# A hybrid layer on one core: weight splits on GpSimd, and another order of work at the start

## The chip, the core and the metric

The kernel runs on one core of a Trainium2 chip. A core has five engines with instruction queues of their own, each of which works its queue strictly in the order in which it was written: TensorE (PE in the profile; its weight loads appear apart as PEld), VectorE (DVE), ScalarE (ACT), GpSimd (POOL) and SyncE (SP), which here only issues transfers. Engines wait for one another through semaphores. The metric is the time of one execution in device microseconds (us), as the median of several runs.

## The reference

One layer, 1024 tokens of width 1024, in fp32. What matters here is the front of it:

```
h    = rmsnorm(x, norm1_w)
proj = h @ w_in                     # all columns of both mixers in one product
q, k, v = silu(causal_conv4(...))   # mixer A: gated delta rule, 4 heads of 128
beta, g = gates from 8 columns of proj
o_a  = rmsnorm(chunked delta rule) * silu(z)
o_b  = dilated attention of 8 heads of 64, three (window, dilation) branches
x    = x + concat(o_a, o_b) @ w_out
x    = x + (silu(gate) * up) @ w_down   # after rmsnorm, up-projection, causal conv of width 3
out  = rmsnorm(x, final_norm_w)
```

## The kernel before

**Layout and precision.** Tensors are kept transposed: 128 partitions by 1024 tokens, eight such tiles for the width. Every large fp32 product is made of three products of TensorE. An operand is split into a high part (`hi`, a rounded copy made by ACT) and a low part (`lo`, source minus high part, made by DVE), and `mm3` (line 200) adds high by high, high by low and low by high into one bank of sums. A row `ps<-xhi,whi` is a product with the high part of an input tile and of a weight, `ps<-xhi,wlo` one with the low part of the weight, `ps<-xlo,whi` one with the low part of the input. Each has 128x512 results.

**Helpers.** `Engine` records every operation, so that all operations of DVE, ACT, POOL and SP have one line in the profile: L142, or L144 if they were written through `uv` or `ua`, which raise their priority in the scheduler by `URGENT`. L193 is a product, L197 a transposition on TensorE. `split` (206) makes a high and a low part with `ac` and `ve`, the handles of normal priority.

**Who sets the order.** TensorE's order is written out by a planner, `Weave`: the parts of the layer are generators, each of which says by `need` when its operands should be ready by modelled costs, and the planner takes the first one that is ready. Every product gets an issue token, so the order stays as planned. The order on the other engines is made by a scheduler, from the dependencies, the place in the program and the priority. `after(inst, anchor)` binds an instruction behind another one without any data between them. Pools have a fixed number of buffers per tag; raw weights (`wst`), their high parts (`whi`) and their low parts (`wlo`) have two each.

**The start** (lines 288 to 324, 346 to 348 and 353 to 361). A loop over the eight row blocks k loads `xt` (block k of the transposed input) and, for every second k, a weight piece, and splits both. Each block is also squared by ACT (`sq`), and DVE adds the squares up in `acc`, which the norm needs. Meanwhile TensorE makes 18 warm-up products that nobody reads. Then `first` makes the columns of three key heads: for each k six groups of three products, into six banks. `norms` (367) sums `acc` over the partitions (`ps<-ones,acc`, 128x1 each) and `gates` (388) makes the gates from eight columns (`ps<-xt,wba`); its last step on DVE is `ngam`. `first_keys` then scales the keys (`xr`), convolves them (`kT<-xr,gcw,kT`) and hands them to `kprep`, which makes the decay matrices `dec` (eight ACT operations a head), the tokens-first copies `ktok` and the small vectors around them.

**The dense stage** (`dense`, 485). It works through `DENSE`, a list of columns: the last key head, two halves of the values of mixer B (`V`), then q and v of each head, eight columns of mixer B (`a`) and four gate columns (`z`). `take` hands out the weight that was split before and starts the split of the next one; weight 0 belongs to the key column, 1 to 8 to the values, 9 to 28 to the other twenty. A value weight is used by eight groups of products with the operands exchanged (`ps<-whi,xhi`, `ps<-wlo,xhi`, `ps<-whi,xlo`, in this order), over four banks, and `vx` on ACT empties the four banks at the end of a half. A column of the other kind takes sixteen groups, 48 products. Woven into this stage are the preparation of q and v (`qT`, `vT`, `vtok`), the forward substitution of the delta rule on DVE (`xi`, `tmp`, `mt`; its result reaches TensorE as `x`, `um`), the chain over the chunks, and the attention of mixer B (scores `ps<-kT,qT`, probabilities `pb`, denominators `rd`). Behind it come the output projection and the MLP, which take most of the time and are not touched.

**POOL before.** It clears some tiles, takes powers (`nk`, `rq`, `ms`), masks `dec`, scales `vtok` and copies `rd`: 78 instructions in all.

The diff touches `weight`, `split_x`, the loop of the start, the warm-up, `first` and `take`:

## Time and profile before

| | us |
|---|---|
| median of three runs (lowest, highest) | 1209.37 (1208.98, 1209.37) |
| the profiled execution | 1209.18 |
| its span in the profile | 1207.4 |
| PE busy | 1192.3 |
| DVE busy | 925.8 |
| ACT busy | 576.2 |
| POOL busy | 59.1 |

The mean clock that TensorE was granted is 0.996 of full speed. The span is the time from the first to the last record; what lies around it, 1.8 us, belongs to the execution and not to any engine. Busy times are sums over records. A row of the timeline gives the start, the length and the tiles of an instruction (or of several alike in a row); products overlap in their records, so the distance between two starts, and not the length, is what one product costs. In brackets stands how long the engine was idle before a row, and which engine's work ended that.

### The profile page before, as it was taken

The numbers are of one execution on the slowest core, as the hardware profiler recorded it, in microseconds if no ns is written. First come the engines' busy times: TensorE is split into PE (matmuls) and PEld (weight loads), VectorE is DVE, ScalarE is ACT, GpSimd is POOL, SyncE is SP. The second block draws the span as 40 slices with busy tenths as digits, with TensorE's granted clock in tenths as the row PEclk, the third lists the DMA queues.
The fourth block names the chain that finished last, engine by engine and source line by source line (L and its number), as shares of the span: only waits on it lengthen the run. The fifth ranks groups of instructions, "written<-read, shape, count | busy, mean of one in ns | idle before, by whom it ended". The sixth has DMA issues, their size and how long they took to land.

```text
span 1207.4 us, 18350 instructions
## 1 busy us (share of the span) xinstructions
PE 1192.3 (99%) x7068; PEld 986.6 (82%) x7068; DVE 925.8 (77%) x1470; ACT 576.2 (48%) x1134; POOL 59.1 (5%) x78
## 2 busy tenths in 40 slices
PE   9999999999999999999999999999999999999997
PEld 7887888889877778888888888888888888888886
DVE  7683975666466556768988989889898889999865
ACT  7384335356355443655545445444454454444441
POOL 0211010003211000000000000000000000000000
PEclk9999999999999999999999999999999999999999
DMA  7424343435633213544223132231322298556513
GB/s 230 111 75 125 117 120 108 157 102 167 213 118 119 89 36 100 174 136 157 71 69 105 53 105 82 75 105 53 105 65 93 89 366 311 177 163 226 162 57 140
DMA packets 85798, 154.80 MB, mean 128 GB/s; under 512 B 21168, under 2 KB 36304, under 8 KB 85712
## 3 DMA queue, kind: packets, MB, share of 16 engines
q1 hardware_dynamic: 85136, 153.12, 39.3%
q8 instruction: 55, 0.90, 0.3%
q10 hardware_dynamic: 576, 0.52, 0.1%
q14 instruction: 31, 0.25, 0.1%
HBM read 117.68 MB, written 35.93 MB: 127 GB/s over the span
## 4 chain that ended last, share of the span: by engine, by line
PE 93%; DVE 3%; ACT 2%; issue 1%; DMA 1%; SPq 0%; POOLq 0%; POOL 0%; DVEq 0%; ACTq 0%
PE ps L193 44%; PE pa L193 20%; PE dw L193 17%; PE pc L193 10%; PE ps L197 3%; DVE kT L142 1%; DMA xt<-in_xT 1%; DVE wlo L142 0%; ACT dec L142 0%; DVE xr L142 0%; DVE x1h L142 0%; PE pd L193 0%; DVE qT L142 0%; SPq L142 0%; ACT xr L142 0%
## 5 line engine op out<-in xcount | busy, mean ns | idle before, releaser
L193 PE MATMUL dw<-pr 128*128 128x512 f32 (+1 forms) x984 | 211.3, 376 | 0.0
L193 PEld LDWEIGHTS dw<-pr 128*128 128x128 f32 x984 | 176.7, 188 | 33.6
L193 PE MATMUL ps<-xhi,whi 128*128 128x512 f32 x384 | 157.3, 410 | 0.0
L193 PE MATMUL ps<-xlo,whi 128*128 128x512 f32 x384 | 150.0, 391 | 0.8 <-DVE xlo L142 0.8
L193 PE MATMUL ps<-xhi,wlo 128*128 128x512 f32 x384 | 150.2, 391 | 0.0
L193 PE MATMUL pa<-T,pair 128*128 128x512 f32 x528 | 127.0, 389 | 0.0
L193 PEld LDWEIGHTS pa<-T,pair 128*128 128x128 f32 x528 | 99.0, 188 | 20.5
L193 PEld LDWEIGHTS ps<-xhi,whi 128*128 128x128 f32 x384 | 72.2, 188 | 18.1 <-issue 4.7
L193 PEld LDWEIGHTS ps<-xhi,wlo 128*128 128x128 f32 x384 | 72.1, 188 | 15.7 <-DVE wlo L142 0.2
L193 PEld LDWEIGHTS ps<-xlo,whi 128*128 128x128 f32 x384 | 72.4, 188 | 13.4 <-DVE xlo L142 1.1
L142 ACT ACTIVATE u<-pa 128x512 f32<-128x512 f32 x44 | 26.3, 598 | 107.3 <-PE pa L193 107.3
L142 DVE SCALAR_TENSOR_TENSOR y<-xu,fcw,y 128x1023 f32<-128x1023 f32 (+1 forms) x44 | 56.4, 1281 | 22.1 <-ACT y L142 22.0
L142 ACT ACTIVATE whi<-wst 128x1024 fp32r<-128x1024 f32 (+2 forms) x33 | 33.3, 1009 | 68.0 <-PE ps L193 62.4
L193 PE MATMUL pa<-B,A 128*128 128x512 f32 x264 | 63.4, 389 | 0.0
L193 PE MATMUL pc<-T,S 128*128 128x512 f32 x264 | 63.4, 389 | 0.0
L193 PE MATMUL pa<-T,S 128*128 128x512 f32 x264 | 63.4, 389 | 0.0
L193 PE MATMUL pc<-B,pair 128*128 128x512 f32 x264 | 63.4, 389 | 0.0
L142 DVE TENSOR_TENSOR wst<-wst 128x512 f32<-128x512 f32 x88 | 60.4, 687 | 0.9
L193 PE MATMUL ps<-B,pair 128*128 128x512 f32 x252 | 60.5, 389 | 0.0
L144 ACT ACTIVATE sm<-sm,mx 128x128 f32<-128x128 f32 (+7 forms) x64 | 35.4, 556 | 50.5 <-DVE mx L144 50.5
L193 PEld LDWEIGHTS pa<-T,S 128*128 128x128 f32 x264 | 49.6, 188 | 10.3
L193 PEld LDWEIGHTS pc<-T,S 128*128 128x128 f32 x264 | 49.6, 188 | 10.3
(245 smaller groups left out, 2344.7 us busy)
## 6 DMA issues: line engine op xcount, KB each, us to landing
wst<-in_wu SPq DMA_DIRECT2D x44, 512.0 KB, 3.7
wd<-in_wd SPq DMA_DIRECT2D x44, 512.0 KB, 4.5
upark<-y SPq DMA_DIRECT2D x22, 512.0 KB, 3.7
wst<-in_wi SPq DMA_DIRECT2D x21, 512.0 KB, 3.7
r<-upark SPq DMA_DIRECT2D x11, 512.0 KB, 7.5
r<-upark SPq DMA_DIRECT2D x22, 256.0 KB, 6.8
wa<-in_wd SPq DMA_DIRECT2D x22, 256.0 KB, 3.1
wst<-in_wv SPq DMA_DIRECT2D x8, 512.0 KB, 3.7
```

Of the source, the lines that this page charges most:

```text
L142: return getattr(eng, op)(*a, **kw)
L144: return getattr(eng, op)(*a, **kw)
L193: tc.stamp_issue_order_token(nc.tensor.matmul(dst, lhs, rhs, start=start, stop=stop, **kw).ins, TOKEN)
L197: tc.stamp_issue_order_token(nc.tensor.transpose(dst, src, ident if idt is None else idt).ins, TOKEN)
```

## The change

It has four parts.

1. `weight` has lost its urgent halves. The value weights (1 to 8) are split whole, at normal priority, on ACT and DVE; the twenty weights from 9 on get their low part from POOL instead of DVE.
2. Ten warm-up products instead of eighteen.
3. In `first`, for the first two row blocks, the two products with the high part of the input come ahead of those with its low part (by groups of three for k=0, over all six for k=1). From k=2 on nothing changes.
4. The splits of the start have raised priority, and every square and its addition into `acc` is bound behind the splits of two row blocks later; the last two behind the last splits.

```
@@ -212,14 +212,16 @@
         sy.dma_start(st, src)
         return st
 
-    def weight(src, n=1024, st=None, urgent=False):
+    def weight(src, n=1024, st=None, spare=False):
         if st is None:
             st = raw_weight(src, n)
         hi = tile_(wp, [P, n], F32R, "whi", "whi", 2)
         lo = tile_(wp, [P, n], F32R, "wlo", "wlo", 2)
-        for sl in (half(0), half(1)) if urgent else (slice(0, n),):
-            (ua if urgent else ac).activation(hi[:, sl], st[:, sl], AF.Copy)
-            (uv if urgent else ve).tensor_tensor(lo[:, sl], st[:, sl], hi[:, sl].bitcast(F32), op=OP.subtract)
+        if spare:
+            ac.activation(hi, st, AF.Copy)
+            po_.tensor_tensor(lo, st, hi.bitcast(F32), op=OP.subtract)
+        else:
+            split(st, hi, lo)
         return hi, lo
 
     def wk_by_halves(src):
@@ -281,9 +283,25 @@
 
     def split_x(xt, k, sl):
         hi, lo = xs[k]
-        ac.activation(hi[:, sl], xt[:, sl], AF.Copy, scale=n1[:, k:k + 1])
-        ve.scalar_tensor_tensor(lo[:, sl], xt[:, sl], n1[:, k:k + 1], hi[:, sl].bitcast(F32), op0=OP.mult,
-                                op1=OP.subtract)
+        his[k:] = [ua.activation(hi[:, sl], xt[:, sl], AF.Copy, scale=n1[:, k:k + 1])]
+        lo_of[0] = uv.scalar_tensor_tensor(lo[:, sl], xt[:, sl], n1[:, k:k + 1], hi[:, sl].bitcast(F32), op0=OP.mult,
+                                           op1=OP.subtract)
+
+    def split_first(src, hi, lo):
+        ua.activation(hi, src, AF.Copy)
+        return uv.tensor_tensor(lo, src, hi.bitcast(F32), op=OP.subtract)
+
+    his, los, lo_of, sqs = [], [], [None], []
+
+    def square(k, hi, lo):
+        sq = A("sq", "qa")
+        late = "the products wait for the splits first"
+        after(ac.activation(sq, xts[k], AF.Square), hi, late)
+        sqs.append(sq)
+        if k == 1:
+            after(ve.tensor_tensor(acc, sqs[0], sq, op=OP.add), lo, late)
+        elif k > 1:
+            after(ve.tensor_tensor(acc, acc, sq, op=OP.add), lo, late)
 
     for k in range(KT):
         xt = A("xt", ("kT*", "dv*")[k % 2])
@@ -299,29 +317,22 @@
             for h in range(2):
                 sy.dma_start(xt[:, half(h)], I["xT"][:P, half(h)])
             sy.dma_start(wst[:, 1, :], I["w0"][0, :, 1])
-            split(wst[:, 0, :], whi[:, 0, :], wlo[:, 0, :])
+            split_first(wst[:, 0, :], whi[:, 0, :], wlo[:, 0, :])
             for h in range(2):
                 split_x(xt, 0, half(h))
-            split(wst[:, 1, :], whi[:, 1, :], wlo[:, 1, :])
+            split_first(wst[:, 1, :], whi[:, 1, :], wlo[:, 1, :])
         else:
             if k % 2 == 0:
                 sy.dma_start(wst, I["w0"][k // 2])
             sy.dma_start(xt, I["xT"][k * P:(k + 1) * P, :])
             if k % 2 == 0:
-                wlast = split(wst, whi, wlo)
+                split_first(wst, whi, wlo)
             split_x(xt, k, slice(0, S))
-        sq = A("sq", "qa")
-        ac.activation(sq, xt, AF.Square)
-        if k == 0:
-            sq0 = sq
-        elif k == 1:
-            ve.tensor_tensor(acc, sq0, sq, op=OP.add)
-        else:
-            inst = ve.tensor_tensor(acc, acc, sq, op=OP.add)
-            if k == 6:
-                after(inst, first_lo, "the products wait for these weights")
-        if k == 4:
-            first_lo = wlast
+        los.append(lo_of[0])
+        if k > 1:
+            square(k - 2, his[k], los[k])
+    for k in (KT - 2, KT - 1):
+        square(k, his[-1], los[-1])
 
 
     ident = const("ident", [P, P], I["ident"])
@@ -344,8 +355,8 @@
 
 
     wbank = bank("atr", "warm")
-    for _ in range(18):
-        mm(wbank[:, :P], warm, warm, 0.3)
+    for _ in range(10):
+        mm(wbank[:, :P], warm, warm, 0.43)
 
 
     pst = [bank(t) for t in ("hf", "asc", "ch") for _ in range(2)]
@@ -353,11 +364,24 @@
     def first():
         for k in range(KT):
             w = wk0[k // 2]
-            for i in range(6) if k else (0, 2, 4, 1, 3, 5):
+            if k < 2:
+                for group in ((0, 2, 4), (1, 3, 5)) if k == 0 else (range(6),):
+                    for low in range(2):
+                        for i in group:
+                            m, h = divmod(i, 2)
+                            wm = [t[:, k % 2, m * P:(m + 1) * P] for t in w]
+                            hi, lo = [t[:, half(h)] for t in xs[k]]
+                            if low:
+                                mm(pst[i], wm[0], lo, 0.2135, False, False)
+                            else:
+                                mm(pst[i], wm[0], hi, 0.2135, k == 0, False)
+                                mm(pst[i], wm[1], hi, 0.2135, False, False)
+                continue
+            for i in range(6):
                 yield wv.need(*xs[k], *w)
                 m, h = divmod(i, 2)
                 wm = [t[:, k % 2, m * P:(m + 1) * P] for t in w]
-                mm3(pst[i], wm, [t[:, half(h)] for t in xs[k]], k == 0, k == KT - 1)
+                mm3(pst[i], wm, [t[:, half(h)] for t in xs[k]], False, k == KT - 1)
         wv.done.add("first")
 
 
@@ -513,7 +537,7 @@
             w = nxt.pop()
             i = place[0] = place[0] + 1
             if i < len(srcs):
-                nxt.append(weight(None, st=raw.pop(), urgent=1 <= i <= 8))
+                nxt.append(weight(None, st=raw.pop(), spare=i >= 9))
             if i + 1 < len(srcs):
                 raw.append(raw_weight(srcs[i + 1]))
             return w
```

What this does to the queues is seen at three places. On DVE at the start, the additions into acc stood each right behind its low part; the rows before:

```order
L142 TENSOR_TENSOR wlo<-wst,whi 128x384
L142 TENSOR_SCALAR xlo<-xt,n_72,xhi 128x512 x2
L142 TENSOR_TENSOR wlo<-wst,whi 128x384
L142 TENSOR_SCALAR xlo<-xt,n_72,xhi 128x1024
L142 TENSOR_TENSOR acc<-sq 128x1024
L142 TENSOR_TENSOR wlo<-wst,whi 128x768
L142 TENSOR_SCALAR xlo<-xt,n_72,xhi 128x1024
L142 TENSOR_TENSOR acc<-acc,sq 128x1024
L142 TENSOR_SCALAR xlo<-xt,n_72,xhi 128x1024
L142 TENSOR_TENSOR acc<-acc,sq 128x1024
L142 TENSOR_SCALAR xlo<-xt,n_72,xhi 128x1024
L142 TENSOR_TENSOR acc<-acc,sq 128x1024
```

and the same place after:

```order
L144 TENSOR_TENSOR wlo<-wst,whi 128x384
L144 TENSOR_SCALAR xlo<-xt,n_72,xhi 128x512 x2
L144 TENSOR_TENSOR wlo<-wst,whi 128x384
L144 TENSOR_SCALAR xlo<-xt,n_72,xhi 128x1024
L144 TENSOR_TENSOR wlo<-wst,whi 128x768
L144 TENSOR_SCALAR xlo<-xt,n_72,xhi 128x1024 x2
L142 TENSOR_TENSOR acc<-sq 128x1024
L144 TENSOR_SCALAR xlo<-xt,n_72,xhi 128x1024
L142 TENSOR_TENSOR acc<-acc,sq 128x1024
L144 TENSOR_SCALAR xlo<-xt,n_72,xhi 128x1024
L142 TENSOR_TENSOR acc<-acc,sq 128x1024
L144 TENSOR_TENSOR wlo<-wst,whi 128x768
```

The first addition has moved behind three further splits, and the others follow two row blocks late.

On ACT, between the two halves of the values (`vx` empties the banks of the first half, `whi` is a weight of the second, `dec`, `eg` and `ge` belong to the last key head), the rows before:

```order
L142 ACTIVATE vx<-ps,rst 128x512 x3
L142 ACTIVATE dec<-dec,ngc 128x128 x5
L144 ACTIVATE whi<-wst 128x512 x2
L142 ACTIVATE dec<-dec,ngc 128x128 x3
L142 ACTIVATE eg<-gend 128x8
L142 ACTIVATE ge<-gel 128x8
L142 ACTIVATE vx<-ps,rst 128x512
```

and after:

```order
L142 ACTIVATE vx<-ps,rst 128x512 x2
L142 ACTIVATE dec<-dec,ngc 128x128 x8
L142 ACTIVATE eg<-gend 128x8
L142 ACTIVATE ge<-gel 128x8
L142 ACTIVATE vx<-ps,rst 128x512 x2
L142 ACTIVATE whi<-wst 128x1024
```

Two of the four vx now stand behind the eight dec, and the weight's high part, whole, stands behind all of them instead of among the dec.

On POOL, from the clearing of `xi` for the forward substitution to the powers for q of the later heads, the rows before:

```order
L142 MEMSET xi 128x1024
L142 AFFINE_SELECT xi<-xi 128x1024
L142 TENSOR_TENSOR rq<-ssq,mhalf 128x8
L142 MEMSET x_1672 128x1024
L142 MEMSET x_1686 128x1024
L142 TENSOR_TENSOR rq<-ssq,mhalf 128x8 x3
```

and after:

```order
L142 MEMSET xi 128x1024
L142 AFFINE_SELECT xi<-xi 128x1024
L142 TENSOR_TENSOR wlo<-wst,whi 128x1024 x4
L142 TENSOR_TENSOR rq<-ssq,mhalf 128x8
L142 TENSOR_TENSOR wlo<-wst,whi 128x1024
L142 MEMSET x_1645 128x1024
L142 MEMSET x_1659 128x1024
L142 TENSOR_TENSOR wlo<-wst,whi 128x1024
L142 TENSOR_TENSOR rq<-ssq,mhalf 128x8
L142 TENSOR_TENSOR wlo<-wst,whi 128x1024 x2
L142 TENSOR_TENSOR rq<-ssq,mhalf 128x8
```

The subtractions stand between the powers and the clearings of x, in one queue with them.

TensorE's own order changes little: apart from the first two row blocks, sixteen groups instead of twenty-six stand as full groups of three ahead of the first gate product because twelve were rewritten, so that the gates and the norm now come two groups (six products) later; one transposition of a key head comes a group earlier, and two of q and v of the last head two groups later or earlier; a few groups change places between steps of the attention. On SP the third weight piece of the start moves ahead of the last block of the input.

## The prediction

> **What bounds the kernel now.** I read the busy shares first, then the timeline of the start in order of time, then the waits of PE, and last the windows of the clock around each wait.
>
> ```profile
> PE 1192.3 (99%) x7068; PEld 986.6 (82%) x7068; DVE 925.8 (77%) x1470; ACT 576.2 (48%) x1134; POOL 59.1 (5%) x78
> ```
>
> PE is busy for 1192.3 us, 99% of the span, and no product is taken out or put in beyond eight warm-up products. So the change can give back only PE's idle time and what PE does slowly, and it can cost only by making PE wait. POOL is nearly free. All sums below are made against the profiled execution, whose own time is 1209.18 us, 0.19 below the median of 1209.37; I add the 0.19 at the end. About 0.2% (2.4 us) is what a measurement of this kernel can tell from no change.
>
> **The start.** Timeline of before; columns are start, length, engine, line, operation, tiles, shapes, and in brackets the idle time and what ended it.
>
> ```profile
> 1.10 5.61 PE L193 MATMUL warm<-warm 128*128 128x128 f32 x36 [1.10 <-DVE ones L142]
> 4.48 0.72 ACT L142 ACTIVATE xhi<-xt,n 128x512 fp32r<-128x512 f32 x1 [0.24 <-DMA xt<-in_xT]
> 6.47 0.48 PE L193 MATMUL ps<-xhi,whi 128*128 128x512 f32 x1
> 7.01 0.73 ACT L142 ACTIVATE xhi<-xt,n 128x512 fp32r<-128x512 f32 x1 [1.80 <-DMA xt<-in_xT]
> 9.41 1.15 ACT L142 ACTIVATE xhi<-xt,n 128x1024 fp32r<-128x1024 f32 x1 [0.32 <-DMA xt<-in_xT]
> 11.94 0.50 PE L193 MATMUL ps<-xlo,whi 128*128 128x512 f32 x1 [0.82 <-DVE xlo L142]
> 13.81 1.28 DVE L142 SCALAR_TENSOR_TENSOR xlo<-xt,n,xhi 128x1024 fp32r<-128x1024 f32 x1
> 15.00 1.22 DVE L142 TENSOR_TENSOR acc<-acc,sq 128x1024 f32<-128x1024 f32 x1
> 15.93 0.39 PE L193 MATMUL ps<-xhi,whi 128*128 128x512 f32 x1
> 30.88 0.61 PE L193 MATMUL ps<-ones,acc 128*128 128x1 f32 x4
> ```
>
> Eighteen warm-up calls leave 36 rows, so ten leave 20, and the warm-up ends between 4.2 (20/36 of 5.61) and 4.9 (the early rows are the slow ones). The first high part of the input ends at 4.48 + 0.72 = 5.20: the first product can start at about 5.25 instead of 6.47. But the next high parts wait for transfers (7.01 and 9.41 are released by the DMA), and the change does not make those earlier. The products of row block k=1 can start when its high part ends, 9.41 + 1.15 = 10.56. Its low part, which made PE wait before 11.94, is now wanted only after twelve products (of about 0.23 us: the first window below has ten rows of PE in 2.30 us), so that wait goes. Eighteen products from 10.65 end near 14.8, and block k=2 starts there instead of at 15.93: a gain of 1.1 us.
>
> Most of it is lost at once. The adds into acc now stand behind later splits on DVE. Rows that follow each other on DVE overlap by 0.08 to 0.09 (13.81 + 1.28 is 15.09, the next starts at 15.00), so an add costs 1.14 and a low part of the input 1.20. From the end of the fourth low part, which by ACT's order is near 16.0, DVE has still to do seven adds (8.0), four low parts (4.8), two weight splits of 768 and one of 1024 columns (together about 2.9, an estimate from the 1231 ns of a 1024 split quoted below, by size and less the overlap) and two small ones (0.3): the last add ends at about 32.0. PE would reach the products of ones and acc two column products later (1.36) and 1.1 earlier, at about 31.1, so it waits 0.9 there and starts them at 32.1 instead of 30.88. With 1.36 us of column products already behind it, PE is then 0.15 ahead. The gates and norms, however, are 1.2 later, and the next row says whom that touches.
>
> **The value stage.** The timeline again, then three windows of 3.41 us (columns after the window: length, busy time and rows of PE, of its weight loads, DVE, ACT, POOL; granted clock, DMA share, GB/s).
>
> ```profile
> 45.51 0.18 DVE L142 TENSOR_SCALAR ngam<-ngam 128x32 f32<-128x32 f32 x1 [1.14 <-ACT ngam L142]
> 46.62 0.69 DVE L142 TENSOR_TENSOR xr<-ps,rstdB 128x512 f32<-128x512 f32 x1 [0.92 <-PE ps L193]
> 72.83 1.18 ACT L144 ACTIVATE whi<-wst 128x512 fp32r<-128x512 f32 x2
> 73.54 0.50 PE L193 MATMUL ps<-whi,xhi 128*128 128x512 f32 x1
> 74.41 1.29 DVE L144 TENSOR_TENSOR wlo<-wst,whi 128x512 fp32r<-128x512 f32 x2
> 75.15 0.50 PE L193 MATMUL ps<-wlo,xhi 128*128 128x512 f32 x1 [1.11 <-DVE wlo L144]
> 88.83 1.88 ACT L142 ACTIVATE vx<-ps,rst 128x512 f32<-128x512 f32 x3
> 90.54 1.62 ACT L142 ACTIVATE dec<-dec,ngc 128x128 f32<-128x128 f32 x5
> 94.12 0.71 ACT L142 ACTIVATE vx<-ps,rst 128x512 f32<-128x512 f32 x1
> 94.89 0.50 PE L193 MATMUL ps<-whi,xhi 128*128 128x512 f32 x1 [2.11 <-ACT vx L142]
> 97.01 0.63 PE L193 MATMUL ps<-whi,xlo 128*128 128x512 f32 x1
> 97.43 0.63 PE L193 MATMUL ps<-whi,xhi 128*128 128x512 f32 x1
> ```
>
> ```profile
> 72.19:75.60 3.41, 2.30 (x10) 1.40 (x9) 3.37 (x4) 3.41 (x17) 0.00 (x0) 1.00 0.00 0
> 92.67:96.08 3.41, 1.30 (x9) 1.02 (x8) 1.29 (x2) 2.16 (x8) 0.00 (x0) 1.00 0.61 73
> 96.08:99.50 3.42, 3.42 (x13) 2.73 (x11) 0.00 (x0) 1.63 (x9) 0.00 (x0) 0.50 0.76 268
> ```
>
> DVE's chain for the keys starts with xr at 46.62. The last gate step, ngam, stands ahead of it at 45.51 and moves to about 46.7, so the keys' chain starts near 46.83: 0.2 later. DVE and ACT run without a pause from there to the values, so 0.2 is carried on.
>
> At 75.15 PE waited for the first half of a weight's low part. The weight is now split whole and at normal priority, at the same place in DVE's row: the low part starts at 74.41 + 0.2 and takes 1.23, where the first half took about 0.65. PE goes on at about 75.9, which costs 0.7. PE's idle time there grows to about 2.3 us: 0.8 until the whole high part is made, then one product, then 1.5. Within the window 72.19 to 75.60 PE would be busy for about 1.3 us, which is what it was in 92.67 to 96.08; that window was followed by one at clock 0.50, in which the products stand 0.42 apart (97.01 to 97.43) instead of 0.23, while 72.19 to 75.60 with 2.30 busy was followed by full speed. So I take it that the clock now falls after 75.6, for one window. Eight or nine products at 0.2 extra are 1.6 us.
>
> At 94.89 PE waited for the fourth vx, which empties a bank. On ACT it stood behind the eight dec and two urgent halves of whi. Now two vx, eight dec, two small ones and two vx follow each other, with whi behind them. The vx stand 0.57 apart and the dec 0.29 (five take 1.62, the last alone 0.46): the first vx at 88.83, the dec from 89.97 to 92.3, the small ones to 92.5, the fourth vx at 93.1 to 93.8, all 0.2 to 0.4 later by the chain. PE's fourth value product of that group starts near 94.1 where it had 94.89. It waited from about 92.7 before; it now arrives at 92.5 (clock kept) or later, idles 1 us at the most, and the window at half speed, 96.08 to 99.50, goes: another 1.6. Where the clock was kept at 75.6, PE is then 0.75 + 1.6 = 2.35 ahead. Where it fell, PE arrives 2.3 later than before at this place, so at about 94.8 with no wait left, and is 1.6 to 1.8 ahead; I take 1.7. The two cases lie only 0.65 apart, since the wait takes up most of what is lost at 75.6.
>
> **Twenty subtractions on POOL.** From groups by line, waits (from 200 to 440 us), the timeline, a window, and the view of one tile (lengths in ns, then first and last start):
>
> ```profile
> L142 DVE TENSOR_TENSOR wlo<-wst,whi 128x1024 fp32r<-128x1024 f32 x23 | 28.3, 1231 | 6.9 <-ACT whi L142 6.8
> L142 POOL TENSOR_TENSOR vtok<-vtok,ms 128x1024 f32<-128x1024 f32 x4 | 7.6, 1897 | 0.3
> PE ps L193 <- DVE vtok L144: 0.3, 1, 0.3
> PE ps L197 <- ACT qT L142: 0.2, 1, 0.2
> 353.72 0.48 PE L193 MATMUL ps<-kT,qT 64*128 64x128 f32 x2
> 355.73 0.50 PE L193 MATMUL ps<-xhi,whi 128*128 128x512 f32 x1
> 382.72 0.48 PE L193 MATMUL ps<-kT,qT 64*128 64x128 f32 x2
> 384.74 0.50 PE L193 MATMUL ps<-xhi,whi 128*128 128x512 f32 x1
> 418.85 0.93 PE L193 MATMUL ps<-kT,qT 64*128 64x128 f32 x8
> 120.00:165.00 45.00, 45.00 (x216) 37.73 (x215) 41.89 (x93) 16.93 (x38) 1.71 (x1) 1.00 0.33 116
> 148.14 1.71 POOL L142 TENSOR_TENSOR rq<-ssq,mhalf 128x8 f32<-128x8 f32 x1 [42.54 <-DVE ssq L142]
> 172.86 1.28 DVE L142 SCALAR_TENSOR_TENSOR vT<-xr,gcw,vT 128x1021 f32<-128x1021 f32 x1
> 172.99 2.65 POOL L142 TENSOR_TENSOR rq<-ssq,mhalf 128x8 f32<-128x8 f32 x1 [3.53 <-DVE ssq L142]
> L193 PE MATMUL ps<-x,um x32: 191/191/212, 193.5 to 194.0; 32*32 32x32 f32 x32
> ```
>
> DVE loses twenty splits, 20 x 1.23 = 24.6 us. POOL has no such row; the nearest is its multiply of the same shape, 1.90 us. A subtraction costs between that and, if it first waits for a DVE operation as rq seems to at 172.99 (2.65 us beside a DVE row of 1.28, where the same operation took 1.71 at 148.14), about 3.2; I take 2. A column takes 48 products, 11 us at 0.23, and its split starts when the column before the last gave its tiles free; less the high part on ACT and the queue, the low part has some 9 us until a product needs it: at 3.2 it is still covered. If that cover went, each further us would be one of PE's idle time.
>
> DVE may be held in turn. The tightest place is forward substitution, where DVE is busy 41.89 of 45 us. Five subtractions fall there; if each holds DVE for its own length, 5 x 1.9 = 9.5 us are added and 5 x 1.23 = 6.2 saved, 3.3 late. The substitution ends by 165, and the products of x and um, which want its result, start at 193.5 behind columns that do not need it; that cover is longer, so I cost it at nothing. On POOL itself the next split stands behind the two clearings of x that wait for the substitution's end; it is 3.3 late with them, within its 9.
>
> What comes back is where DVE's split stood ahead of something PE wanted. The group of eight score products takes 355.73 - 353.72 = 2.01 us and 384.74 - 382.72 = 2.02 where a split precedes the copies of pb on DVE, and 0.93 at 418.85 where none does: 1.1 each, 2.2 in all. The waits for vtok (0.3) and qT (0.2; two column products more now stand ahead of it) add 0.5. Together 2.7. The bounds are 0, if the groups are slow for another reason, and 3.5, which grants 0.8 for delays of the same kind that no row here names. In attention POOL also makes rd; a copy behind a subtraction is 2 us late, and is wanted only one round of score products later, so I cost it at nothing. The few column products that change places between attention's steps are no work added.
>
> **Sum.** Start 0.15 (spent again by the wait at 75), value stage -1.7 with the clock falling at 75.6, POOL -2.7: 4.4 off 1209.18 is 1204.8, and with the 0.19 it is 1205.0 us.
>
> **Rivals.** *The clock does not fall at 75.6.* The window may lie otherwise by a few tenths, or 1.3 busy may not be the mark. Then -2.35 - 2.7: 1204.3 us. The Trainium skill, "TensorE: Matmul & The Clock Gate", Practical rules, says that one whole window without work brings half speed, and asks for no gap above about 3 us; by that rule a gap of 1.5 costs no clock, and the time is this rival's. The trace speaks against it: the window 92.67 to 96.08, with 1.30 us of work in it, was followed by half speed.
>
> *POOL gives nothing back.* The subtractions block DVE for as long as the splits did, or pb was late by itself. Then only the value stage's 1.7 to 2.35 remains, 1207.0 to 1207.7, in the middle 1207.4 us, within 0.2%. For it speaks the rq row; against it that pb is copied from a bank of sums and has only one operand in SBUF, if any.
>
> *The subtractions starve (slower).* Beside a DVE that is busy 93% of 120 to 165, a POOL subtraction might get only the time that DVE leaves, and take far longer than 1.9. It decides at 9 us: four columns lie there, and at 12 us each the low part is 3 late four times, so PE waits 12 and the time is 1209.4 - 4.4 + 12 = 1217 us; at 10.1 the gains are just used up. For it: no row here shows POOL at work on a large tile beside a full DVE; against it: rq lost 0.9 us beside a two-operand DVE row, less than that row's length. The Trainium skill, "SBUF — State Buffer", Who interferes with whom, says that a DVE instruction with two SBUF inputs and a GpSimd instruction that reads SBUF exclude each other, each for the whole instruction, whichever starts first. The rq rows agree with that; by it a subtraction waits for one DVE row and then runs through, so about 3.2 us at the most, which is covered.
>
> *The start's loss comes through.* If acc ends later than 32.0, or the halves taken away stop PE at more weights than the one at 75, the value stage gives 0.8 of loss instead of 1.7 of gain: -2.7 + 0.8, 1207.5 us.
>
> **Chances.** Forecast 0.38; no fall of the clock 0.27; POOL gives nothing 0.16; the start's loss comes through 0.07; slower 0.12. The first two and 0.02 of the others are faster by over 0.2% (0.67), 0.21 lies within, 0.12 slower. The range runs from 1202.6 (no fall of the clock, POOL's upper bound, and PE not waiting 0.9 for acc) to 1209.4 (POOL's and the start's gains both gone); it leaves out the slow rival and some 0.05 below. The likeliest case's own range, by POOL's bounds of about 2 and 3.5, is 1204.2 to 1205.7.
>
> **What would show it.** The first product near 5.25 and block k=2 near 14.8; ones and acc near 32.1 after a wait of 0.9; the low part at 75 waited for until 75.9 and a window at clock 0.5 right after it; no wait above 1 us at 94 and full clock at 96 to 99.5; DVE's wlo from 23 rows of 1024 to about 11 with POOL's twenty near 2 us; the two score groups near 0.9 us. I am wrong if POOL's subtractions run over 9 us, if PE waits for x and um near 193, if a new wait for wlo stands in the columns, or if another window falls to half speed.

## The result, and where the time went

The changed kernel takes 1206.16 us (median of 12 runs, 1204.92 to 1206.93), and the kernel before takes 1208.13 us beside it (12 runs, 1206.42 to 1209.37). The ratio is 0.9981, with a 95% interval of 0.9973 to 0.9988: a small gain of 2.3 us by this ratio and of 2.0 us by the two medians. The forecast was 4.4 us.

The profiled execution after has a span of 1204.7 us, where before it was 1207.4. PE is as full as it was, and POOL has taken over 49 us:

```profile
span 1204.7 us, 18295 instructions
PE 1189.1 (99%) x7052; PEld 983.3 (82%) x7052; DVE 917.7 (76%) x1442; ACT 575.3 (48%) x1126; POOL 107.7 (9%) x98
```

DVE is only 8 us less busy, although twenty splits of 1.23 us (24.6 us) were taken from it. So some 16 us of DVE's rows have become longer. The waits of PE after, longest first (us in all, times, longest):

```profile
PE ps L197 <- DVE at L142: 1.5, 1, 1.5
PE ps L193 <- DVE wlo L142: 1.1, 1, 1.1
PE warm L193 <- DVE ones L142: 1.1, 1, 1.1
PE ps L197 <- POOL rs L142: 1.1, 1, 1.1
PE ps L193 <- DVE acc L142: 0.9, 1, 0.9
PE ps L193 <- ACT xhi L144: 0.5, 1, 0.5
PE ps L193 <- DVE xr L142: 0.5, 1, 0.5
```

The wait of 2.1 us for vx is gone, and so are those for pb. The waits for acc and xhi are new and were foreseen. Those for `at` (1.5 us) and for `xr` (0.5 us) are new and were not.

The start of one and the same product in the two traces (matched by its place among the products of its form) shows where PE gains and loses:

| product | before, us | after, us | lead, us |
|---|---|---|---|
| the first one | 6.47 | 5.40 | 1.07 |
| row block 2 | 15.93 | 14.74 | 1.19 |
| the value group that waits for wlo | 73.54 | 73.47 | 0.08 |
| the value group that waited for vx | 94.89 | 92.77 | 2.12 |
| three groups later | 99.42 | 95.63 | 3.79 |
| a column in forward substitution | 137.18 | 133.59 | 3.59 |
| a column near its end | 155.66 | 155.37 | 0.30 |
| a column of the chain over chunks | 230.39 | 228.98 | 1.40 |
| a column near the second group of scores | 384.74 | 381.22 | 3.52 |
| a column near the end of the splits | 405.27 | 401.59 | 3.67 |
| output projection, first product | 475.81 | 472.75 | 3.05 |

The start gives nothing that lasts. The value stage gives 3.7 us, forward substitution takes 3.3 back, and the rest of the dense stage gives 3.4, of which it loses 0.6 again behind 405 us, where a few groups stand in another order. The cause of that last piece is open.

**The value stage** after, in time order:

```profile
31.99 0.35 PE L193 MATMUL ps<-ones,acc 128*128 128x1 f32 x2 [0.90 <-DVE acc L142]
46.59 0.18 DVE L142 TENSOR_SCALAR ngam<-ngam 128x32 f32<-128x32 f32 x1 [1.14 <-ACT ngam L142]
46.69 3.08 DVE L142 TENSOR_TENSOR xr<-ps,rstdB 128x512 f32<-128x512 f32 x5
73.82 1.22 DVE L142 TENSOR_TENSOR wlo<-wst,whi 128x1024 fp32r<-128x1024 f32 x1
75.10 0.50 PE L193 MATMUL ps<-wlo,xhi 128*128 128x512 f32 x1 [1.13 <-DVE wlo L142]
87.49 1.34 ACT L142 ACTIVATE vx<-ps,rst 128x512 f32<-128x512 f32 x2
88.62 2.51 ACT L142 ACTIVATE dec<-dec,ngc 128x128 f32<-128x128 f32 x8
91.16 1.32 ACT L142 ACTIVATE vx<-ps,rst 128x512 f32<-128x512 f32 x2
92.30 1.13 ACT L142 ACTIVATE whi<-wst 128x1024 fp32r<-128x1024 f32 x1
```

The products of ones and acc start at 31.99 after a wait of 0.90, and ngam stands at 46.59: both as forecast. But the keys' chain is not later for it. The same row before reads:

```profile
46.62 3.41 DVE L142 TENSOR_TENSOR xr<-ps,rstdB 128x512 f32<-128x512 f32 x5 [0.92 <-PE ps L193]
```

Before, DVE was idle for 0.92 us ahead of xr, and the five started 0.68 apart. After, they follow ngam at once and start 0.60 apart. Started 0.07 later, they end 0.26 earlier. By 73.82 the low part starts 0.6 earlier than the 74.41 of before, so that the whole split delays PE no more than the half did. Not all of the 0.6 is the order of the start. Another 0.23 is gained between 51 and 59 us, where four convolutions of the keys on DVE run beside POOL's masks of `dec`. A convolution takes 1.28 us, but 1.5 or 2.1 where it meets a mask, and the masks start when a DMA lands. The rows before:

```profile
51.74 7.59 DVE L142 SCALAR_TENSOR_TENSOR kT<-xr,gcw,kT 128x1023 f32<-128x1023 f32 x4
54.74 3.51 POOL L142 TENSOR_SCALAR_AFFINE_SELECT dec<-dec 128x1024 f32<-128x1024 f32 x2 [0.55 <-DMA dec<-gdram]
```

and after:

```profile
51.47 7.36 DVE L142 SCALAR_TENSOR_TENSOR kT<-xr,gcw,kT 128x1023 f32<-128x1023 f32 x4
```

In three profiles whose code is the same up to this place (two of the kernel before, and one of the experiment "POOL's part alone" below) the low part starts at 74.41, 74.04 and 74.31. In the two kernels below that have whole splits and the start of before it starts at 73.84 and 74.41. So a good part of the 0.6 is what one execution differs by from the next.

**Forward substitution** after: the rows of POOL and DVE, and then PE's waits.

```profile
118.77 0.30 DVE L142 TENSOR_TENSOR tmp<-mt,xi 128x135 f32<-128x135 f32 x1
118.97 2.39 POOL L142 TENSOR_TENSOR wlo<-wst,whi 128x1024 fp32r<-128x1024 f32 x1 [3.62 <-ACT whi L142]
119.11 2.42 DVE L142 TENSOR_TENSOR xi<-xi,tmp 128x135 f32<-128x135 f32 x1
129.10 2.63 POOL L142 TENSOR_TENSOR wlo<-wst,whi 128x1024 fp32r<-128x1024 f32 x1 [7.74 <-ACT whi L142]
129.51 2.50 DVE L142 TENSOR_TENSOR tmp<-mt,xi 128x255 f32<-128x255 f32 x1
142.55 2.42 POOL L142 TENSOR_TENSOR wlo<-wst,whi 128x1024 fp32r<-128x1024 f32 x1 [10.81 <-ACT whi L142]
143.16 2.05 DVE L142 TENSOR_TENSOR xi<-xi,tmp 128x220 f32<-128x220 f32 x1
139.84 0.47 PE L193 MATMUL ps<-xhi,whi 128*128 128x512 f32 x1 [0.51 <-DVE xr L142]
152.85 0.63 PE L197 MATMUL ps<-ident,vT 128*128 128x128 f32 x4 [0.18 <-DVE gq L142]
154.96 0.44 PE L197 MATMUL ps<-ident,vT 128*128 128x128 f32 x2 [1.47 <-DVE at L142]
```

A row of 128x135 takes 0.30 us at 118.77, and 2.42 at 119.11, where it meets a subtraction that started 0.14 earlier on POOL: it ends 0.17 after POOL does. The same happens at 129.51 and 143.16. A row that reads only one tile of SBUF, the memory of the tiles, is not held. An xr, whose other operand is a bank of sums, starts 0.01 after the third subtraction and takes its usual 0.68 us; the row behind it, which reads two tiles, is the one that is held:

```profile
142.56 0.68 DVE L142 TENSOR_TENSOR xr<-ps,rstdB 128x512 f32<-128x512 f32 x1
```

Against their lengths elsewhere (0.30, 0.42 and 0.38) the three rows lose 5.9 us on DVE, for three splits that would have cost 3.7. In DVE's one queue the convolutions of q and v, the scaling `xr` that empties a bank for PE, and `at` stand behind these rows.

**Attention** after, the two score groups and what follows them:

```profile
351.49 0.93 PE L193 MATMUL ps<-kT,qT 64*128 64x128 f32 x8
352.34 0.50 PE L193 MATMUL ps<-xhi,whi 128*128 128x512 f32 x1
379.57 0.93 PE L193 MATMUL ps<-kT,qT 64*128 64x128 f32 x8
380.42 0.50 PE L193 MATMUL ps<-xhi,whi 128*128 128x512 f32 x1
```

Each takes 0.85 us from start to start, where it was 2.01 and 2.02.

### The profile page after: what moved, and what is told of

It reads as the page before. It is cut to its first block, busy times and chain, and to the rows that moved or that the text cites. A ratio compares the mean times of both kernels' runs of the same rounds, so it can differ in the third digit from the quotient of the medians.

```text
span 1204.7 us, 18295 instructions
## 1 busy us (share of the span) xinstructions
PE 1189.1 (99%) x7052; PEld 983.3 (82%) x7052; DVE 917.7 (76%) x1442; ACT 575.3 (48%) x1126; POOL 107.7 (9%) x98
## 4 chain that ended last, share of the span: by engine, by line
PE 88%; DVE 7%; issue 2%; DMA 1%; ACT 1%; SPq 1%; POOLq 0%; POOL 0%; DVEq 0%; ACTq 0%
PE ps L193 38%; PE pa L193 20%; PE dw L193 17%; PE pc L193 10%; PE ps L197 2%; DVE xi L142 1%; DVE kT L142 1%; DVE tmp L142 1%; DMA xt<-in_xT 1%; DVE xr L142 1%; DVE acc L142 1%; SPq L142 1%; ACT sm L144 0%; DVE qT L142 0%; DVE vT L142 0%
## 5 line engine op out<-in xcount | busy, mean ns | idle before, releaser
L142 ACT ACTIVATE whi<-wst 128x1024 fp32r<-128x1024 f32 x36 | 38.4, 1065 | 73.2 <-PE ps L193 47.3
L142 POOL TENSOR_TENSOR rs<-rs,mhalf 128x2 f32<-128x2 f32 (+2 forms) x4 | 4.5, 1115 | 738.8 <-DVE rs L144 738.8
L142 POOL TENSOR_TENSOR wlo<-wst,whi 128x1024 fp32r<-128x1024 f32 x20 | 47.9, 2396 | 123.5 <-ACT whi L142 121.7
```

Source lines behind the costliest of these rows:

```text
L142: return getattr(eng, op)(*a, **kw)
```

## The experiments

The theory at this point: the changed kernel is the sum of a gain in the value stage that comes from the whole splits alone, of a loss in forward substitution because POOL holds DVE while it subtracts, of a gain behind it because DVE is free, and of a start that is worth nothing. Rivals for the loss: DVE's order, which the scheduler has changed there too; or that PE, 3.8 us ahead, simply runs into a stage that DVE bounds. In the comparisons below "before" always is the kernel before, run on the same chip beside the others of its group.

**Clear instead of subtract.** Only what POOL does for three weights changes; all queues stay in the order of the changed kernel. The low parts of these weights are left out of the products.

```
-            po_.tensor_tensor(lo, st, hi.bitcast(F32), op=OP.subtract)
+            if clear:
+                po_.memset(lo.bitcast(F32), 0.0)
+            else:
+                po_.tensor_tensor(lo, st, hi.bitcast(F32), op=OP.subtract)
...
-                nxt.append(weight(None, st=raw.pop(), spare=i >= 9))
+                nxt.append(weight(None, st=raw.pop(), spare=i >= 9, clear=10 <= i <= 12))
```

> The changed kernel, but for the weights 10, 11 and 12 POOL clears the low part instead of subtracting (the low part of these three weights is left out of the result). Every engine's order stays as it is; POOL's instruction no longer reads SBUF. Theory (a subtraction on POOL holds DVE for its whole length during forward substitution): the DVE rows of 2.42, 2.50 and 2.05 us go back to about 0.4, PE's waits at 139.8, 152.9 and 155.0 go, and the time falls by about 3 us to 1203. Rival one (DVE's order puts the convolutions of q and v too late) and rival two (PE simply comes 3.8 us early to a stage that DVE bounds): the waits stay within 0.5 us of what they are, and so does the time, 1206.

Measured: 1202.84 us, ratio to before 0.9953 (0.9940 to 0.9965). The stretch from 117 to 158 us of the two traces, first after, then this kernel (columns: length; busy time and rows of PE, its weight loads, DVE, ACT, POOL; clock, DMA share, GB/s):

```profile
117.00:158.00 41.00, 38.67 (x183) 31.13 (x183) 39.35 (x84) 14.68 (x35) 10.30 (x4) 1.00 0.34 109
```

```profile
117.00:158.00 41.00, 41.00 (x198) 34.41 (x197) 36.06 (x84) 16.02 (x36) 8.63 (x6) 1.00 0.39 130
```

PE goes from 38.67 to 41.00 busy of 41.00: its waits there are gone. POOL works on tiles of the same size at the same places in its queue, but only writes (and starts 0.7 to 3.3 us earlier, since a clear waits for no high part):

```profile
117.20 0.95 POOL L142 MEMSET wlo<- 128x1024 f32 x1 [1.71 <-PE ps L193]
128.37 0.96 POOL L142 MEMSET wlo<- 128x1024 f32 x1 [10.21 <-PE ps L193]
139.25 0.96 POOL L142 MEMSET wlo<- 128x1024 f32 x1 [9.92 <-PE ps L193]
```

The product near the end of the stage that stood at 155.37 stands at 152.01, 3.4 us earlier. With every queue in the same order, neither rival can explain that. It shows that the subtractions of these three weights cost the 3.3 us that PE loses in this stage. Nor is it only that a clear is shorter (0.96 us against 2.4). Within the first clear, 117.20 to 118.15, DVE's rows of the same kind run on in their usual time:

```profile
117.23 0.23 DVE L142 TENSOR_TENSOR xi<-xi,tmp 128x60 f32<-128x60 f32 x1
117.50 0.25 DVE L142 TENSOR_TENSOR tmp<-mt,xi 128x87 f32<-128x87 f32 x1
117.78 0.25 DVE L142 TENSOR_TENSOR xi<-xi,tmp 128x87 f32<-128x87 f32 x1
```

So a clear does not hold DVE at all, and a subtraction, which also reads two tiles, does. The Trainium skill, "SBUF — State Buffer", Who interferes with whom, says that a DVE instruction with two SBUF inputs and a GpSimd instruction that reads SBUF exclude each other for the whole instruction, and that one that only writes does not contend; the traces agree with both.

**Those three weights on DVE, the others on POOL.**

```
-                nxt.append(weight(None, st=raw.pop(), spare=i >= 9))
+                nxt.append(weight(None, st=raw.pop(), spare=i == 9 or i >= 13))
```

> The changed kernel with the low parts of weights 10, 11 and 12 on DVE again, all others as changed. Theory: no DVE row is held, three splits of 1.2 us come back to DVE, 3 us of PE's waits go: 1203.3 us. Rival two (DVE bounds the stage): DVE has as much to do as with the holds, less 2.4 us, so at least 1 us of the waits stays: 1204.5 or more.

Measured: 1203.23 us, ratio 0.9955 (0.9942 to 0.9967), 2.9 below the changed kernel's median. The stretch from 117 to 158 us:

```profile
117.00:158.00 41.00, 41.00 (x199) 34.39 (x198) 38.27 (x86) 16.38 (x37) 4.12 (x2) 1.00 0.32 104
```

PE has no idle time there although DVE makes the three splits itself. Rival two falls: with PE as far ahead as in the changed kernel, DVE keeps up.

**No low part on POOL.**

```
-                nxt.append(weight(None, st=raw.pop(), spare=i >= 9))
+                nxt.append(weight(None, st=raw.pop(), spare=False))
```

> The changed kernel with all low parts on DVE; the start and the whole splits of the value weights stay. Theory: the waits of forward substitution go (-3.3), the two groups of score products go back to about 2.0 us and the waits at 222 and 264 return (+2.6): about 1205.5 us. Rival two: the waits of forward substitution stay, 1208.5 us.

Measured: 1205.56 us, ratio 0.9976 (0.9967 to 0.9985). Its trace loses nothing in forward substitution (3.4 us ahead of before at both ends of it) and gains nothing behind it (3.5 us at the output projection). By the medians POOL's seventeen other subtractions are thus worth 2.3 us (1205.56 to 1203.23). All twenty together are worth nothing that the runs can tell: the changed kernel's ratio of 0.9981 is not better than this 0.9976.

**POOL's part alone**, on the kernel before.

```
+        if spare:
+            ac.activation(hi, st, AF.Copy)
+            po_.tensor_tensor(lo, st, hi.bitcast(F32), op=OP.subtract)
+            return hi, lo
...
-                nxt.append(weight(None, st=raw.pop(), urgent=1 <= i <= 8))
+                nxt.append(weight(None, st=raw.pop(), urgent=1 <= i <= 8, spare=i >= 9))
```

> The kernel before with the twenty low parts from weight 9 on made by POOL, and nothing else. PE comes to forward substitution 3.8 us later than in the changed kernel, because it still waits for vx near 95. Theory (POOL holds DVE, and what PE loses by it is what its lead over DVE's row is worth): of the 3.3 us at most 1 stays, the two score groups and the waits at 222 and 264 give 2.4, and the time is 1.5 to 2.5 us below before, about 1206.7. Rival (the loss in forward substitution is POOL's price alone, wherever PE stands): +3.3 - 2.4, about 1 us above before, 1209.7.

Measured: 1210.28 us beside 1209.33, ratio 1.0006 (0.9997 to 1.0015). The expected gain did not come; the time cannot be told from that of before, and the rival, which put it about 1 us higher, was the nearer. PE's waits are here again, a little elsewhere:

```profile
150.86 1.16 PE L193 MATMUL ps<-qT,kT 128*128 128x128 f32 x8 [1.27 <-ACT sq L144]
158.52 0.66 PE L197 MATMUL ps<-ident,vT 128*128 128x128 f32 x4 [1.04 <-DVE at L142]
```

The column that stood at 155.66 before stands at 158.94: 3.3 us lost. In this trace PE (by 3.5 us) and the held rows of DVE's substitution (the first two by 3.7 and 3.9 us) both come later than in the changed kernel, so that PE's place gives DVE no slack. With no other part of the change present, the price is POOL's, and what comes back later (2.7 us to the output projection) does not cover it.

**Whole splits of the value weights alone**, on the kernel before.

```
-                nxt.append(weight(None, st=raw.pop(), urgent=1 <= i <= 8))
+                nxt.append(weight(None, st=raw.pop(), urgent=False))
```

> The kernel before with only the value weights (1 to 8) split whole and at normal priority. Theory (the value stage's gain comes from ACT's order alone): the wait of 2.1 us for vx near 94.9 goes, and PE is 2 to 4 us ahead of before at the end of the values; nothing else changes, so 2 to 4 us less than before, about 1205 us. Rival (the earlier keys' chain or the start's order is needed for it): within 1 us of before.

Measured: 1206.07 us, ratio 0.9974 (0.9965 to 0.9983). In its trace the fourth value group starts at 92.80 instead of 94.89, and the lead of 3.8 us over the profiled execution of before lasts to the end. The value stage's gain needs neither the start nor POOL. Part of it comes from a place that I had not looked at. ACT before:

```profile
76.92 1.24 ACT L144 ACTIVATE whi<-wst 128x512 fp32r<-128x512 f32 x2
77.96 1.15 ACT L142 ACTIVATE xr<-kT 128x1024 f32<-128x1024 f32 x1
81.33 2.46 ACT L142 ACTIVATE dec<-dec,ngc 128x128 f32<-128x128 f32 x8 [2.23 <-DVE gel L142]
```

and in the changed kernel:

```profile
76.24 1.15 ACT L142 ACTIVATE xr<-kT 128x1024 f32<-128x1024 f32 x1
77.19 1.15 ACT L142 ACTIVATE whi<-wst 128x1024 fp32r<-128x1024 f32 x1
78.76 2.45 ACT L142 ACTIVATE dec<-dec,ngc 128x128 f32<-128x128 f32 x8 [0.43 <-DVE gel L142]
```

The urgent halves stood ahead of the keys' xr; without the urgency xr goes first, and this head's dec come 2.6 us earlier. With that, ACT reaches the vx at 87.49 and not, as I had it, at 88.83 and later; how much of the gain this brings, and how much the place of whi behind the vx, was not separated.

**The start alone**, on the kernel before: ten warm-up products, high parts first, raised priority of the splits, squares bound late (parts 2 to 4 of the change as they are), with `weight` and `take` of before. In `take`, against the changed kernel, this is:

```
-                nxt.append(weight(None, st=raw.pop(), spare=i >= 9))
+                nxt.append(weight(None, st=raw.pop(), urgent=1 <= i <= 8))
```

> The kernel before with the start of the changed one alone (ten warm-up products, high parts first, splits of raised priority, squares late); halves for the value weights and DVE for all low parts as before. Theory (the start's gain of 1.1 us is taken back by the wait for acc): PE ahead by 1 us at row block 2, by 0.3 or less at 45 us, and within 0.5 us of before in all. Rival (the earlier start carries through): 1 us or more below before.

Measured: 1208.17 us beside 1208.97, ratio 0.9995 (0.9986 to 1.0004): no difference that can be told. Its trace leads by 1.4 at row block 2 and by 0.5 at 45.7 us.

**No change of the start**: the changed kernel with the loop of the start, the warm-up and `first` of before, and with POOL's part as in the second experiment.

```
-    for _ in range(10):
-        mm(wbank[:, :P], warm, warm, 0.43)
+    for _ in range(18):
+        mm(wbank[:, :P], warm, warm, 0.3)
...
-                nxt.append(weight(None, st=raw.pop(), spare=i >= 9))
+                nxt.append(weight(None, st=raw.pop(), spare=i == 9 or i >= 13))
```

> The changed kernel without its start (the start as in the kernel before, eighteen warm-up products) and with the low parts of weights 10, 11 and 12 on DVE: only what has shown a gain so far. Theory (the start is worth nothing or costs some tenths): 1202.7 to 1203.3 us, level with the same kernel that has the new start (1203.23). Rival (the start helps by about 1 us once nothing behind it is slower): 1204.2 us.

Measured: 1202.72 us (1202.52 to 1205.53), ratio 0.9953 (0.9939 to 0.9966), level with 1203.23 for the same with the new start. These two beat both kernels, by some 3 us the changed one, and they differ from each other by nothing that the runs can tell.

**Squares free**, in the kernel of the second experiment.

```
-        after(ac.activation(sq, xts[k], AF.Square), hi, late)
+        ac.activation(sq, xts[k], AF.Square)
...
-            after(ve.tensor_tensor(acc, acc, sq, op=OP.add), lo, late)
+            ve.tensor_tensor(acc, acc, sq, op=OP.add)
...
-        if k > 1:
-            square(k - 2, his[k], los[k])
-    for k in (KT - 2, KT - 1):
-        square(k, his[-1], los[-1])
+        square(k, his[k], los[k])
```

> The changed kernel with the low parts of weights 10, 11 and 12 on DVE and the squares not bound behind later splits (they stand where the scheduler puts them). Theory: acc is ready before PE wants it, the wait of 0.9 us before the products of ones and acc goes, but the wait for the low part near 75 takes the same time back if the keys' chain does not start earlier; since the gates' last step comes 0.7 to 1.2 us earlier too, about 0.5 us of it stays: 1202.7 us. Rival (squares ahead of splits make the first products wait instead): 1203.2 or more.

Measured: 1204.43 us, ratio 0.9963 (0.9951 to 0.9976). Its interval overlaps that of the kernel with the squares bound (0.9955, 0.9942 to 0.9967), but the traces agree with the medians: level at 23 us, 2.1 us behind that kernel at 28, and 1.2 behind from 35 us on to the output projection. That fits the rival:

```profile
25.79 0.50 PE L193 MATMUL ps<-xhi,wlo 128*128 128x512 f32 x1 [1.77 <-DVE wlo L144]
```

The squares and their additions now delay the third weight piece, and PE waits 1.8 us for its low part. Late squares cost 0.9 us at acc and save that; together with the earlier first products the two come out at nothing.

**The kernel before, once more**, with no edit.

> The kernel before, unchanged, for a second profile. Theory (the window at half speed after the wait near 94.9 depends on how the clock's windows lie against the program): where the first window at full speed starts at another time than 3.92 us, the half-speed window is gone or begins at another place, and the time is some 1.5 us less or the same, while the wait for vx stays 2.1 us. Rival (it belongs to the wait): a half-speed window begins within 1.5 us after the wait again.

Measured: 1207.55 us in one run, span 1205.8. The windows of this profile around the wait for vx, and the product that waits:

```profile
90.04:93.45 3.41, 2.35 (x12) 1.61 (x10) 2.67 (x9) 3.41 (x11) 0.57 (x1) 1.00 0.54 173
93.45:96.87 3.42, 2.34 (x12) 2.00 (x13) 0.20 (x1) 1.93 (x9) 0.00 (x0) 1.00 0.75 165
96.87:100.28 3.41, 3.41 (x21) 2.89 (x21) 0.69 (x4) 3.22 (x17) 0.51 (x1) 1.00 0.45 165
```

```profile
94.53 0.50 PE L193 MATMUL ps<-whi,xhi 128*128 128x512 f32 x1 [2.14 <-ACT vx L142]
```

The wait is the same 2.14 us, and the run is 1.6 us shorter than the profiled execution of before. But a window ends at 93.45, in its midst, each of the two windows has 2.3 us of work, and the clock stays at 1.00. In the profile shown of before one window (92.67 to 96.08) held nearly all of the wait, and half speed followed. That is what the theory had. Two more kernels on record have this wait. Their profiles go with it: POOL's part alone waits 2.14 us within one window (92.83 to 96.24, 1.45 us of work), the start alone 2.13 us (91.84 to 95.25, 1.28 us of work), and in both the next window is at half speed.

## Why the prediction was right, and where it was off

The direction was right, and the measured time of 1206.16 us lies in the stated range, which reached from 1202.6 to no change at all. Of the gain of 4.4 us about half came. That it still landed there is in part luck: against the profile of before the value stage brought 2.1 us more than forecast, forward substitution took 3.3 that stood in the sum at nothing, and the base was 1.2 too high.

- *The start, 0.15 us, nothing that lasts:* right. The wait for acc came at 31.99 with 0.90 us, as worked out; alone, the start is worth 0.9995 of the time, not to be told from 1.
- *The keys' chain 0.2 us later:* wrong. The five xr started 0.07 later and ended 0.26 earlier, and the chain came 0.6 earlier at 73.82, in part by chance, as said above. I had taken the start of the first of five rows as what sets the chain, and I had read DVE as running without a pause from there, where it waits for ACT several times, for up to 1.48 us.
- *PE goes on at 75.9 and the clock falls:* wrong by both. PE went on at 75.10, after 1.7 us of idle time in place of 2.3, and no half-speed window followed in the profile. There the idle time is shared by two windows, which is luck; but with all low parts on DVE one window (72.28 to 75.69) holds it and keeps 2.13 us of work, and the clock stays at 1.00 there too. The nearest case was the rival without the fall.
- *The wait for vx goes, and PE is 1.7 ahead (2.35 without the fall):* right in mechanism, too small in size; it was 3.8. Of this, 2.1 us come at the product that had waited for vx, where I had 0.75, and 1.7 behind it with the half-speed window, where I had 1.6. I had left ACT's earlier order as it was and missed that the halves had stood ahead of the keys' xr. PE's arrival "at 92.5 (clock kept)" also left out the 0.7 lost at 75; the sum does not hang on it, since it goes by the time of vx.
- *POOL: 2.7 us back:* right in mechanism and nearly in size. From the end of forward substitution to 405 us PE gains 3.4 us, the two score groups 1.16 us each; without POOL's seventeen others the time is 2.3 higher. A subtraction took 2.39 us and not 2.
- *Forward substitution at nothing:* this is the step that failed, and it is what the other half of the gain went into: 3.3 us. I had seen the hold, and its size per subtraction was nearly right (1.9 us; 1.7 to 2.1 were measured), but three subtractions fall into the stage and not five, and they make DVE 2.2 us late. That the 3.3 worked out there for DVE is also what PE lost is chance. I had then asked only when PE wants the end of the substitution, near 193. But DVE's queue there also holds the convolutions of q and v, the xr that free banks and at, which PE wants within a few us. The cover of the last result was not the cover of the rows that stand between. The profile of before could have warned me: the prediction says that no row shows POOL at work on a large tile beside a full DVE, but between 50.92 and 58.25 us POOL masks the 128x1024 tile `dec` four times while DVE is busy without a gap, and three of the four convolutions there take 2.10 us instead of 1.28.
- The base was also off. The profiled execution of before held a window at half speed that is not in every execution of that kernel; the twelve runs beside the changed kernel, the three that I started from among them, have a median of 1208.13, 1.2 below that of the three. Of the 3.8 us in the value stage some 1.6 stand only against executions with that window: against the second profile of before it is 2.2.

Of the rivals, "the subtractions starve" did not come: none took over 2.7 us in the stage. But the time by which DVE waits for POOL, which I had priced beside it and called hidden, was the cost.

## What to carry to other kernels

Work that is moved to an idle engine is not free for the engine that it is taken from: look at whether the two can run at the same time on the operands at hand, and take as price the whole length on the slower engine in each place where the faster one has no idle time (here 2 us held for 1.2 us saved). Move it where the first engine has gaps, and leave it where it has none; that split gave 2.9 us more than moving all of it. And when an engine is made late, go through every row of its queue for who waits for it, not only the last.

## What the runs showed of the hardware

The granted clock changes in steps of 3.413 us: the first stretch at full speed lasts 92.16 us, 27 such windows, in the profile of before, and 88.75 us, 26 of them, in that of the start alone. The window at half speed after an idle time of PE depends on how that idle time lies in the windows. The same wait of 2.1 us was followed by half speed where one window kept 1.28, 1.30 or 1.45 us of work, and not where it was shared between two with 2.35 and 2.34. Windows with 1.76 us (152.68 to 156.09, the changed kernel) and 1.65 us (22.53 to 25.95, squares free) of work were not followed by half speed. Busy time alone is not the mark, though: at the end of the changed kernel's trace, where PE makes smaller products, a window with 2.53 us (1193.74 to 1197.16) was. In eleven profiles the first window at full speed began anywhere between 3.9 and 7.1 us of the span, in the two of the kernel before at 3.92 and 4.71, so which of the two happens is not set by the kernel alone. The runs of the kernel before spread over 1206.3 to 1211.1 us, and those of the changed kernel, which has no such wait, over 1204.9 to 1206.9. That the window accounts for the whole of the spread was not shown: the kernel of the experiment "No change of the start", which has no such wait either, spread over 1202.5 to 1205.5, and its longest run, with a mean clock of 0.995 where the others had 0.997 or 0.998, has no profile.

The Trainium skill, "TensorE: Matmul & The Clock Gate", Why this matters for your kernels, puts the loss of the full clock at one whole window of idle time; here windows with 1.28 to 1.45 us of work in 3.41 were enough.

A subtraction of 128x1024 on POOL took 2.39 us, where a multiplication of a tile of that size by a spread-out small one (vtok by ms) took 1.90.
